# Experts with few tokens on 32 slots, chosen by a branch for each weight matrix

## The chip, the core and the metric

The kernel runs on one core of a Trainium2 chip. The metric is the device time of one execution in microseconds (us), the median of several runs. A profiled execution gives the trace that all the rows below are read from. TensorE (PE in the rows, with its weight loads as PEld) multiplies matrices into PSUM; VectorE (DVE) and ScalarE (ACT) do the work on elements; SyncE (SP) issues the transfers of weights on the DMA engines; GpSimd (POOL) does little here.

## What is computed

Two blocks over 256 tokens of width 1024, all in fp32. The first has a mixer (a short convolution and two kinds of attention) and then a mixture of 32 experts with the four best for each token; the second has a convolution and Fourier mixer, two feed-forward layers and a pooling mixer. The change lies in the experts alone:

```python
logits = (xt @ router_w + router_b).astype(jnp.float32)
top_vals, top_idx = lax.top_k(logits, TOP_K)              # 4 of 32 experts
top_w = jax.nn.softmax(top_vals, axis=-1)
combine = jnp.einsum('tk,tke->et', top_w, one_hot(top_idx, N_EXPERTS))
def expert_step(acc, params):
    w1, b1, w2, b2, gate_e = params                       # w1 [1024, 2048], w2 [1024, 1024]
    u = xt @ w1 + b1
    glu = jnp.minimum(u[:, ::2], SWIGLU_LIMIT)
    lin = jnp.clip(u[:, 1::2], -SWIGLU_LIMIT, SWIGLU_LIMIT)
    a = glu * jax.nn.sigmoid(SWIGLU_ALPHA * glu) * (lin + 1)
    return acc + gate_e[:, None] * (a @ w2 + b2), None
```

The reference runs every expert over all tokens. The kernel runs an expert over its own tokens: these are gathered into slots by a one-hot matrix, and the results are scattered back, times their weights.

## The kernel before

**Weights.** All weights come as a stream of tiles of 1 MB (8 KB on each of 128 partitions) through 19 slots (`Ring`, the loads issued at L139 on SyncE's queue). `ring.take()` hands out the next tile, `ring.release(item)` frees its slot and issues the load that takes it; that load waits on SyncE's queue until the last matmul that reads the slot is done. An expert has 12 tiles: 8 of w1, 4 of w2. So the tile 19 places further on is issued when a tile is released.

**Slots.** The main path takes the first 64 tokens of an expert (`C = 64`). `w1_mm` (L994, the bias at L999) multiplies them with the first matrix: the 64 columns of slots fill half of TensorE's columns, so two chunks of 512 weights run beside each other in two column groups; each of the 8 tiles is released when its matmuls are done (`free(k)`). `glu` (L1008 to L1012, VectorE and ScalarE) works on two banks of PSUM. `w2_mm` transposes (L1016), copies the result on ScalarE (L1017), and multiplies with the second matrix (L1026), again in two column groups, with a release for each tile.

**More than 64 tokens.** A branch on the expert's count, `tc.If(cv_e > C)` at L1139, runs the first half of a narrow path for up to 32 more tokens (`narrow_a`: `gather1` L958, `w1_mm` with n=32, `glu` of one bank), and inside it a further branch (`wide`, L1083) for more than 96. The second half (`narrow_b`, with `w2_mm32`: L1034, L1035, L1041) stands behind the branch at L1159. For the 32 slots the matmuls run in four column groups. Expert after expert all of this is written out, so the code of the skipped paths lies between. The counts are read into registers of TensorE, ScalarE and VectorE (`count`, L985).

**Order in an expert.** The branch at L1139; `gated` of the expert before (L1046 to L1048); the one-hot matrices of the next pair of experts (L952) where the expert is the first of a pair; first matrix; `glu`; the scatter of the expert before (L1055); its own scatter matrix (`scat_mat`: L973, L975, copies L976 on ScalarE and `gc` L977 on VectorE); the branch at L1159; transposes; half of the next pair's gather (`gather2`, L967, into the bank that `scat_mat` used), given to `w2_mm` as `fill`, so that it runs while ScalarE copies; second matrix. Each engine runs its own list in this order and waits on semaphores. In the last expert 10 released slots go to buffers of the second block and not to the stream.

Of the kernel before, what the change touches and what calls it, by code (L numbers as in the profile page):

```python
# [23 lines left out]
KO = (0, 2, 4, 6, 1, 3, 5, 7)  # neighbours from different banks of PSUM  # L24
# [5 lines left out]
# order of the steps of the first mixer  # L30
# [7 lines left out]
# column packs: name -> (offset, width)  # L38
# [16 lines left out]
NCOL1 = _COLS["conv_w2"][0]  # the columns before are for the first block alone  # L55
# [55 lines left out]
NKEEP = _COFF["tri_gt"][0]  # the rest is for the first block alone  # L111


class Ring:
    """a stream of weight tiles through 8 KB slots; a slot is a tag of a pool"""
# [31 lines left out]
    def release(self, item):  # L147
        """the slot takes the next load, unless a claim on slots is open"""
        if self.claim:
            self.claim -= 1  # L150
            self.claimed.append(item[0])
        else:
            self.free.append(item[0])
        self.pump()


def block_kernel(tc, a, out):
# [7 lines left out]
    # ------------------------------------------------------------------ weight stream  # L165
# [38 lines left out]
    # the last tile comes in two loads, so that its first rows are used while the others come  # L204
# [27 lines left out]
    # ------------------------------------------------------------------ resident data  # L232
# [39 lines left out]
    class Split:  # L272
        """next weight tile in two halves, each as high and low part in fp32r"""
# [37 lines left out]
    def cols_mm(ps, halves, xh, xl):  # L311
        """ps[b] = (128 columns of half b)^T x, tokens along the free axis"""
        for b, (hi, lo) in enumerate(halves):
            h3, l3 = (w.rearrange("p (k n) -> p k n", k=KT) for w in (hi, lo))
            for k in KO:
                mm3(ps[b], h3[:, k, :], l3[:, k, :], xh[:, k, :], xl[:, k, :], k == KO[0], k == KO[-1])

    def pair_mm(acc, yh, yl, kp, halves, first, last, ts=(0, 1), hs=(0, 1)):
        """acc[t][h] += y[:, tile 2 kp + j]^T (row tile j of the pair)"""
# [13 lines left out]
    # ------------------------------------------------------------------ first block: modulation, h  # L333
# [40 lines left out]
    # weights of the forget gate, padded to 32 columns  # L374
# [66 lines left out]
    # ------------------------------------------------------------------ mixer  # L441
    v_row = ap_.tile([P, 2, 768], F32, name="v_row")
    # log f of the six heads from columns 0 and 64 on
    lf = tp_.tile([P, 2, 2, 64], F32, name="lf")
    cumq = tp_.tile([P, 2, 8], F32, name="cumq")
    # queries and keys of the two heads of a pair, each on its 64 partitions; on the others a head's
    # row is chosen on the queries' side and the sums of -log f of all heads are on the keys'
# [23 lines left out]
    def head_rstd(sq, ms, n):  # L471
        """1 / rms over the 64 rows of a head, in place of the squares"""
# [23 lines left out]
    # 384 wide score tiles. stick breaking, [key, query]: 0..255 keys 0..127 against all queries,  # L496
    # 256..383 keys 128..255 against queries 128..255. forgetting, [query, key]: 0..127 the first
    # query tile against its keys, 128..383 the second against all.
# [105 lines left out]
    def fx_z(i):  # L604
# [6 lines left out]
        mk = con("mask_qk")  # of 128 keys before and the query tile's own  # L611
# [19 lines left out]
    def fx_t(i):  # L631
        """to [key, query]: 0..255 keys 0..127, 256..383 keys 128..255 of queries 128..255"""
# [49 lines left out]
    def group(g, b):  # L682
        """half b of a group of columns (of rows, for the values)"""
# [21 lines left out]
    # ------------------------------------------------------------------ output projection  # L705
# [27 lines left out]
    def row_cols(src, j0):  # L733
        """rows j0 and j0 + 1 of src, features along the partitions"""
# [9 lines left out]
    def router_cols():  # L744
        """the second norm's shift, repeated, and its gain, features along the partitions"""
# [4 lines left out]
    def router_bias(s2b, gain):  # L750
        """what the shift adds to the router's bias; the router's weights times the gain"""
# [49 lines left out]
    # ------------------------------------------------------------------ residual, second norm, router  # L801
# [7 lines left out]
    cnt = mp.tile([P, NE], I32, name="cnt")  # L809
    gate1, shift2 = rowt[:, 0, :], rowt[:, 1, :]  # L810
# [36 lines left out]
    def logits(t, hTs):  # L847
        """x times the router's weights, these times the rows' gain; 1 / rms and the rest come later"""
# [12 lines left out]
    def top4(t):  # L861
        """the largest four of a row of logits, and the exponentials"""
# [42 lines left out]
    dve.tensor_copy(cnt, pos[:, 2, :])  # L905
    act.preload_act_table_set(SET_SIG)
# [5 lines left out]
    # ------------------------------------------------------------------ experts  # L912
# [9 lines left out]
    # the halves of b2 from partitions 0 and 64 on  # L922
# [16 lines left out]
    GT_x = mo.tile([P, T], F32R, name="GT_x")  # L939
    U = mps.tile([P, 2, 512], F32, name="U")  # L940
# [3 lines left out]
    def one_hot(S, e, base, n=C):  # L944
        """token -> slot from base on, laid out 128 / n times"""
# [15 lines left out]
    def gather2(Sp, xg, q, bank=bank0):  # L961
        """row tiles 4q .. 4q+3 for two experts at once; Sp: [token, expert, t, (copy, slot)]"""
# [25 lines left out]
    def w1_mm(sel, w1s, xg, n=C, free=None):  # L988
        """u of n slots: chunk j of 512 columns on the partitions from n * (j % (128 / n)) on"""
        m = P // n  # L990
        for k in range(KT):
# [9 lines left out]
            if free:  # L1001
                free(k)

    def glu(nb, l):
        """of nb banks of u"""
# [8 lines left out]
    def w2_mm(av, w2s, ps, o_ps, free=None, fill=None):  # L1014
# [3 lines left out]
        if fill:  # L1018
            fill()
        a4 = aT_t.rearrange("p (b j c) -> p b j c", b=4, j=2)  # L1020
        for kk in range(KT):
            # hidden tile kk belongs to chunk n = kk // 2, half hb = kk % 2
# [5 lines left out]
            if free and hb:  # L1028
                free(KT + n)

    def w2_mm32(av, w2s, ps, o_ps):
        """32 slots; even and odd hidden tiles summed on partitions of their own"""
# [11 lines left out]
    def gated(o_ps, t32, gc, oh, ol):  # L1044
        """times the weights of the slots and the second gate, in two parts"""
# [11 lines left out]
    def pair_hot(p):  # L1057
        """one-hot matrices of experts 2p and 2p + 1"""
        Sp = S_all[p % 2]
        for i in range(2):  # L1060
            one_hot(Sp[:, i], 2 * p + i, 0)
        return Sp

    def bias2():
        """the gated rows of b2, weighted as the experts' outputs are"""
# [14 lines left out]
    # The first 64 tokens of an expert take the main path. Up to 32 more take a narrow one, in two  # L1080
    # steps around the main path's, and the rest goes 64 at a time.
# [25 lines left out]
    def diagonals():  # L1107
        """diag(w_j) for the taps of the second block's convolution that TensorE takes"""
# [12 lines left out]

    Sp = pair_hot(0)
# [8 lines left out]
    for e in range(NE):  # L1131
# [7 lines left out]
        with tc.If(cv_e > C):  # L1139
            # one-hot matrices that are free: the next pair's before they are made, this pair's first after its use  # L1140
            S_x = S_all[(p + 1 - b) % 2][:, 0]
            wide(C + 32, cv_e, e, S_x, sel, w1s, w2s, Oh[b], Ol[b])
            narrow_a(e, S_x, sel, w1s)
# [6 lines left out]
        w1_mm(sel, w1s, lambda k: xg2[p % 2][:, k, b, :], free=lambda i: ring.release(items[i]))  # L1150
        glu(2, l_t)
# [7 lines left out]
        with tc.If(cv_e > C):  # L1159
            narrow_b(w2s, Oh[b], Ol[b])  # L1160
        fill = (lambda: gather2(Sp, xg2[(p + 1) % 2], b)) if 2 * (p + 1) < NE else None
        w2_mm(l_t, w2s, bank1, bank1, free=lambda i: ring.release(items[i]), fill=fill)
# [469 lines left out]
```

## Time and profile before

| | us |
|---|---|
| median of 3 runs | 1738.89 |
| lowest and highest | 1734.43, 1739.25 |
| span of the profiled execution | 1734.7 |
| TensorE, busy time in it | 1583.5 |
| DMA engines, mean share over the span | 0.77 for the main queue |

The span runs from the first to the last instruction of the profiled execution; a run's time is taken from outside it. The experts take about 1020 us of the span: the first matmul of expert 0 starts at 215.1 us, and expert 31's last one ends near 1235. In the rows a busy engine is one that has an instruction under way; a name such as `U<-w,M` says what is written and read, and "128*64" with a matmul is rows times columns of the array that it uses. A letter q behind an engine (PEldq, SPq) marks its sequencer, which decodes, branches and waits.

### The profile page before, as it was taken

Reading aid. Unit: us, or ns where it says so; the run is one execution under the profiler, and the core shown is the slowest. Engines: PE = TensorE matmul, PEld = TensorE weight load, DVE = VectorE, ACT = ScalarE, POOL = GpSimd, SP = SyncE. Lnnn points to the kernel's source line nnn. Section 1 sums busy time; section 2 is a strip of 40 time slices with the busy share of each in tenths; the row PEclk is TensorE's granted clock in tenths of the full one; section 3 lists DMA queues with packets and bytes.
Section 4 is the critical chain, followed back from the end, with each engine's and each line's share of the span. In section 5 each row is a group of like instructions: output and inputs, shape, how many; then the busy total and the mean of one; then the engine's idle time right before and its main releaser. Section 6 shows DMA issues by size and latency. Waiting matters only on the chain. (4 is left out here: it accounts for less than half of the span.)

```text
span 1734.7 us, 22326 instructions
## 1 busy us (share of the span) xinstructions
PE 1583.5 (91%) x9214; PEld 955.0 (55%) x9214; DVE 576.2 (33%) x968; ACT 417.7 (24%) x660; POOL 68.9 (4%) x53
## 2 busy tenths in 40 slices
PE   5999899888989898989989899898889999999998
PEld 2877634343433333433334344343585999989997
DVE  3457401111111111021111111111496655566454
ACT  3465201000100101010101001010534543464343
POOL 0000200000000000000000000000110000200000
PEclk8999999989999999899999999999999999999999
DMA  9568899968999999969999999999224545445430
GB/s 395 229 246 316 321 354 415 414 281 322 414 414 414 417 415 415 393 268 387 416 414 414 416 392 416 415 414 408 108 97 170 214 154 216 154 161 213 178 122 25
DMA packets 95330, 535.44 MB, mean 309 GB/s; under 512 B 8352, under 2 KB 8864, under 8 KB 50976
## 3 DMA queue, kind: packets, MB, share of 16 engines
q1 hardware_dynamic: 94240, 531.37, 76.7%
q8 instruction: 142, 2.33, 0.5%
q10 hardware_dynamic: 896, 1.31, 0.2%
q14 instruction: 52, 0.43, 0.1%
HBM read 531.60 MB, written 1.05 MB: 307 GB/s over the span
## 5 line engine op out<-in xcount | busy, mean ns | idle before, releaser
L994 PE MATMUL U<-w,M 128*64 128x512 f32 (+1 forms) x2176 | 487.8, 619 | 63.9 <-PEq L1139 54.7
L994 PEld LDWEIGHTS U<-w,M 128*64 128x64 f32 (+1 forms) x2176 | 172.9, 140 | 374.6 <-issue 367.9
L1026 PE MATMUL misc<-w,aT_t 128*64 128x512 f32 x1024 | 229.5, 601 | 1.5 <-ACT aT_t L1017 0.8
L292 DVE TENSOR_TENSOR whl<-w,whl 128x1024 fp32r<-128x1024 f32 x168 | 204.2, 1272 | 54.8 <-ACT whl L289 54.7
L309 PE MATMUL G<-hTh,whl 128*128 128x256 f32 x720 | 201.5, 280 | 0.8 <-DVE whl L292 0.8
L307 PE MATMUL G<-hTh,whl 128*128 128x256 f32 x720 | 201.6, 280 | 0.1
L308 PE MATMUL G<-hTl,whl 128*128 128x256 f32 x720 | 201.2, 279 | 0.0
L289 ACT ACTIVATE whl<-w 128x1024 fp32r<-128x1024 f32 x174 | 169.8, 1045 | 21.8 <-DMA w<-in_w_in_dram 19.2
L1008 DVE TENSOR_SCALAR M<-U 128x512 f32<-128x512 f32 (+1 forms) x34 | 23.0, 676 | 444.3 <-PE U L994 427.7
L1026 PEld LDWEIGHTS misc<-w,aT_t 128*64 128x64 f32 x1024 | 71.3, 138 | 135.8 <-issue 128.7
L1009 ACT ACTIVATE M<-M 128x512 f32<-128x512 f32 (+1 forms) x34 | 21.0, 618 | 509.2 <-DVE M L1008 509.2
L1046 DVE SCALAR_TENSOR_TENSOR M<-misc,gc,g2hc 128x512 f32<-128x512 f32 x32 | 24.0, 751 | 340.1 <-PEq L1139 333.4
L307 PEld LDWEIGHTS G<-hTh,whl 128*128 128x128 f32 x720 | 135.7, 188 | 1.2 <-ACT whl L289 0.3
L309 PEld LDWEIGHTS G<-hTh,whl 128*128 128x128 f32 x720 | 135.6, 188 | 1.0 <-DVE whl L292 1.0
L308 PEld LDWEIGHTS G<-hTl,whl 128*128 128x128 f32 x720 | 135.6, 188 | 0.8
L1047 ACT ACTIVATE OO<-M 128x512 fp32r<-128x512 f32 x34 | 21.4, 630 | 283.5 <-DVE M L1046 283.5
L307 PE MATMUL Y<-hTh,whl 128*128 128x256 f32 x224 | 66.5, 297 | 6.8 <-DVE hTh L437 6.1
L309 PE MATMUL Y<-whl,gl 128*128 128x512 f32 x176 | 69.7, 396 | 0.8 <-DVE gl L1463 0.8
L307 PE MATMUL Y<-whl,gh 128*128 128x512 f32 x176 | 69.6, 395 | 0.3 <-ACT gh L1462 0.3
L308 PE MATMUL Y<-whl,gh 128*128 128x512 f32 x176 | 69.5, 395 | 0.0
L308 PE MATMUL Y<-hTl,whl 128*128 128x256 f32 x224 | 65.8, 294 | 0.7 <-DVE hTl L1235 0.7
L967 PE MATMUL misc<-S,h 128*128 128x128 f32 x512 | 65.0, 283 | 0.0
(380 smaller groups left out, 1653.8 us busy)
## 6 DMA issues: line engine op xcount, KB each, us to landing
w<-in_w_dram SPq DMA_DIRECT2D x383, 1024.0 KB, 11.6
w<-in_w_ada_dram SPq DMA_DIRECT2D x24, 1024.0 KB, 9.9
w<-in_w_gate_dram SPq DMA_DIRECT2D x22, 1024.0 KB, 5.0
w<-in_w_up_dram SPq DMA_DIRECT2D x22, 1024.0 KB, 5.4
w<-in_w_down_dram SPq DMA_DIRECT2D x22, 1024.0 KB, 5.1
w<-in_w_in_dram SPq DMA_DIRECT2D x12, 1024.0 KB, 16.4
w<-in_w_ab_dram SPq DMA_DIRECT2D x6, 1024.0 KB, 14.5
w<-in_w_out_dram SPq DMA_DIRECT2D x4, 1024.0 KB, 10.8
```

The costliest lines, as they stand in the source:

```text
L289: act.activation(self.t[j][:, 0, :], src, AF.Copy)
L292: engine.tensor_tensor(self.t[j][:, 1, :], self.w[:, 1024 * j:1024 * (j + 1)], self.t[j][:, 0, :].bitcast(F32), ALU.subtract)
L307: pe.matmul(ps, lh, rh, start=start, stop=False)
L308: pe.matmul(ps, lh, rl, start=False, stop=False)
L309: pe.matmul(ps, ll, rh, start=False, stop=stop)
L967: pe.matmul(ps[:, k], h2[:, t, kk * P:(kk + 1) * P], Sp[:, :, t, 0:C], start=(t == 0), stop=(t == 1))
L994: pe.matmul(U[o:o + n, j // m, :], xg(k), w1s[k][:, 512 * j:512 * (j + 1)], start=(k == 0), stop=(k == KT - 1), tile_position=(0, o))
L1008: dve.tensor_scalar(g, uv[:, :, :, 0], 7.0, None, ALU.min)
L1009: act.activation(s_, g, AF.Sigmoid, scale=1.702)
L1026: pe.matmul(o_ps[C * h:C * h + C, :], lhs, w2s[n][:, hb, 512 * h:512 * (h + 1)], start=(kk == 0), stop=(kk == KT - 1), tile_position=(0, C ...
L1046: dve.scalar_tensor_tensor(t32, o_ps, gc, g2hc, ALU.mult, ALU.mult)
L1047: act.activation(oh, t32, AF.Copy)
```

## The change

An expert with at most 32 tokens runs both of its matrices on 32 slots in four column groups, with the functions that the narrow path already had (`w1_mm` with n=32, `glu` of one bank, `w2_mm32`). The choice is a branch for each matrix, `tc.If(cv_e > 32)` with an `Else`, on TensorE, ScalarE and VectorE; the branch for over 64 tokens moves inside it. The tiles of a matrix are released behind the branch, all together. `gather2` stands ahead of the second branch and not between the transposes and the second matrix. The one-hot matrices lay out the slots of such an expert four times 32 and not twice 64 (`slot_of`). The narrow path has a one-hot matrix of its own (`S_x`). Comments were taken out elsewhere.

```diff
+    few = mp.tile([P, NE], F32, name="few")
...
+    dve.tensor_scalar(few, pos[:, 2, :], 32.5, -32.0, ALU.is_lt, ALU.mult)
...
+    S_x = mo.tile([P, 2, P], F32, name="S_x")
+    upper = mo.tile([P, P], F32, name="upper")
+    slot_of = mo.tile([P, P], F32, name="slot_of")
...
-    def w1_mm(sel, w1s, xg, n=C, free=None):
+    def w1_mm(sel, w1s, xg, n=C):
...
-            if free:
-                free(k)
...
-    def w2_mm(av, w2s, ps, o_ps, free=None, fill=None):
+    def w2_mm(av, w2s, ps, o_ps):
...
-        if fill:
-            fill()
...
-            if free and hb:
-                free(KT + n)
...
         for i in range(2):
-            one_hot(Sp[:, i], 2 * p + i, 0)
+            e = 2 * p + i
+            dve.scalar_tensor_tensor(slot_of, upper, few[:, e:e + 1], iota, ALU.mult, ALU.add)
+            for t in range(2):
+                dve.tensor_scalar(Sp[:, i, t, :], slot_of, posm[:, t, e:e + 1], None, ALU.is_equal)
...
+    dve.tensor_scalar(upper, iota, 31.5, None, ALU.is_gt)
...
-        with tc.If(cv_e > C):
-            S_x = S_all[(p + 1 - b) % 2][:, 0]
-            wide(C + 32, cv_e, e, S_x, sel, w1s, w2s, Oh[b], Ol[b])
-            narrow_a(e, S_x, sel, w1s)
         if e > 0:
             gated(*done)
...
-        w1_mm(sel, w1s, lambda k: xg2[p % 2][:, k, b, :], free=lambda i: ring.release(items[i]))
-        glu(2, l_t)
+        xg_e = xg2[p % 2][:, :, b, :]
+        with tc.If(cv_e > 32) as many:
+            with tc.If(cv_e > C):
+                wide(C + 32, cv_e, e, S_x, sel, w1s, w2s, Oh[b], Ol[b])
+                narrow_a(e, S_x, sel, w1s)
+            w1_mm(sel, w1s, lambda k: xg_e[:, k, :])
+            glu(2, l_t)
+        with many.Else():
+            w1_mm(sel, w1s, lambda k: xg_e[:, k, 0:32], 32)
+            glu(1, l_t)
+        for it in items[:8]:
+            ring.release(it)
...
-        with tc.If(cv_e > C):
-            narrow_b(w2s, Oh[b], Ol[b])
-        fill = (lambda: gather2(Sp, xg2[(p + 1) % 2], b)) if 2 * (p + 1) < NE else None
-        w2_mm(l_t, w2s, bank1, bank1, free=lambda i: ring.release(items[i]), fill=fill)
+        if 2 * (p + 1) < NE:
+            gather2(Sp, xg2[(p + 1) % 2], b)
+        with tc.If(cv_e > 32) as many:
+            with tc.If(cv_e > C):
+                narrow_b(w2s, Oh[b], Ol[b])
+            w2_mm(l_t, w2s, bank1, bank1)
+        with many.Else():
+            w2_mm32(l_t, w2s, bank1, bank1)
+        for it in items[8:]:
+            ring.release(it)
```

## Rows read from the trace of the kernel before

**Rows 1.** The page's first line: the span.

```profile
span 1734.7 us, 22326 instructions
```

**Rows 2.** The page, span in 40 slices: DMA busy tenths, GB/s of each.

```profile
DMA  9568899968999999969999999999224545445430
GB/s 395 229 246 316 321 354 415 414 281 322 414 414 414 417 415 415 393 268 387 416 414 414 416 392 416 415 414 408 108 97 170 214 154 216 154 161 213 178 122 25
```

**Rows 3.** Windows: stretch, length, engines' busy us (instructions), then PEclk, DMA share, GB/s.

```profile
360.00:380.00 20.00, 17.09 (x84) 10.22 (x84) 0.64 (x3) 0.77 (x2) 0.00 (x0) 0.66 0.81 331
460.00:660.00 200.00, 181.50 (x942) 76.66 (x940) 30.93 (x66) 19.24 (x34) 0.00 (x0) 0.99 1.02 415
842.00:1166.00 324.00, 294.40 (x1487) 124.39 (x1484) 51.62 (x109) 30.68 (x56) 0.00 (x0) 0.97 1.01 412
```

**Rows 4.** Waits: waiter <- releaser: us in total, times, longest; 240 to 1250, SyncE's whole.

```profile
PE U L994 <- DMA w<-in_w_dram: 4.0, 2, 2.0
...
SPq L139 <- PE U L994: 470.9, 244, 24.3
```

**Rows 5.** The loads issued at L139, from 200 to 1210 us.

```profile
DMA to landing us min/median/max: 4.8/11.8/20.1
```

**Rows 6.** Timeline of TensorE, expert 4: start, length, line, work [idle before <- releaser].

```profile
336.11 12.24 PE L994 MATMUL U<-w,M 128*64 128x512 f32 x56 [1.89 <-PEq L1139]
...
349.29 1.94 PE L994 MATMUL U<-w,M 128*64 128x512 f32 x8
351.16 1.19 PE L1055 MATMUL Y<-OO,GT 64*128 64x512 f32 x8
...
352.75 0.41 PE L975 MATMUL misc<-cst,S 128*128 128x128 f32 x2
354.15 0.66 PE L1016 MATMUL misc<-cst,M 128*128 128x128 f32 x4 [0.99 <-DVE M L1012]
354.64 1.95 PE L967 MATMUL misc<-S,h 128*128 128x128 f32 x16
356.52 7.09 PE L1026 MATMUL misc<-w,aT_t 128*64 128x512 f32 x32
```

**Rows 7.** Timeline of TensorE: narrow second matrix of expert 5; first matmuls of expert 6.

```profile
405.55 3.64 PE L1041 MATMUL misc<-w,aT_t 128*32 128x512 f32 x32 [0.47 <-ACT aT_t L1035]
...
423.87 0.87 PE L994 MATMUL U<-w,M 128*64 128x512 f32 x2 [1.98 <-DMA w<-in_w_dram]
```

**Rows 8.** Instructions of the branch lines: duration ns min/median/max, first and last start us.

```profile
L1139 PEldq COMPARE_BRANCH  x34: 70/6062/6665, 208.2 to 1200.1; - x34
L1139 PEldq EVENT_SEMAPHORE  x30: 51/51/51, 214.9 to 1206.2; - x30
...
L1159 PEldq COMPARE_BRANCH  x34: 78/332/373, 229.8 to 1221.8; - x34
...
L1083 PEldq COMPARE_BRANCH  x2: 6064/6154/6243, 359.3 to 715.5; - x2
```

**Rows 9.** Timeline of VectorE: experts 4 (two banks) and 5 (one bank).

```profile
353.40 0.69 DVE L1012 TENSOR_TENSOR M<-M 128x512 f32<-128x512 f32 x1
354.01 0.19 DVE L981 COPY sel<-cst 128x64 f32<-128x64 f32 x1
354.11 0.15 DVE L977 COPY gc<-misc 128x1 f32<-128x1 f32 x1
...
385.56 0.42 DVE L1008 TENSOR_SCALAR M<-U 128x256 f32<-128x256 f32 x1 [10.01 <-PE U L994]
...
387.26 0.42 DVE L1012 TENSOR_TENSOR M<-M 128x256 f32<-128x256 f32 x1 [0.49 <-DVE M L1011]
```

**Rows 10.** Timeline of TensorE: first expert's first matrix, last expert's second matrix.

```profile
215.14 14.32 PE L994 MATMUL U<-w,M 128*64 128x512 f32 x56 [4.83 <-PEq L1139]
...
1228.01 7.09 PE L1026 MATMUL misc<-w,aT_t 128*64 128x512 f32 x32 [0.75 <-ACT aT_t L1017]
```

## The prediction

> **What bounds the kernel now.** I read the span first [rows 1], then the DMA lines of the page [rows 2]: from the sixth to the 28th of 40 slices, some 1000 us, the queues move about 415 GB/s with all engines full, but for two dips. That is the expert stage, and it looks like a stream of weights that nothing in the arithmetic can shorten. The windows say the same [rows 3]: 415 and 412 GB/s in two long undisturbed stretches, so a tile of 1.049 MB comes every 2.53 to 2.55 us and an expert's 12 tiles every 30.4 to 30.6 us.
>
> The waits correct this [rows 4]. TensorE lost 4.0 us in all to weights that had not landed, while SyncE's queue stood 470.9 us behind the first matrix's matmuls (L994) alone, waiting for slots to come free. A tile takes a median of 11.8 us from issue to landing [rows 5], hence four or five of the 19 slots are in flight and the rest hold landed tiles. TensorE is the bound, and the stream is only just slower than it: a usual expert, read from one start of L994 to the next idle gap, takes 336.11 to 363.61, then 1.89 us idle [rows 6]: 27.5 + 1.9 = 29.4 us against 30.5 for its tiles. TensorE stays behind the stream because each of the two experts with over 64 tokens throws it back by some 30 us (the second matrix ends at 363.61, the next expert starts at 423.9 [rows 7]; during that the queues fall to 331 GB/s [rows 3]).
>
> So two floors lie close together. Whatever TensorE saves pays until the stream is the bound.
>
> How many experts change path can't be read from the trace. I evaluated the reference's router on its inputs: 19 experts have at most 32 tokens, 13 have more, two of these over 64 (65 and 81, experts 5 and 16), and the trace shows the narrow path exactly twice (L1083 x2 [rows 8]).
>
> **Cost of a small expert (at most 32).** Its matmuls exist already, in the narrow path. The second matrix for 32 slots took 3.64 us [rows 7] instead of 7.09 [rows 6], at full clock. The first has twice the records: 2 x 3.64 = 7.3, with its bias 0.9 more, 8.2 us instead of 15.1 (336.11 to 351.23). Behind it the order changes: the gather of the next pair (`gather2`, 1.95) now stands ahead of the branch, and its bank is free only when `gc` is copied, which VectorE does after `glu`. One bank of `glu` ends 2.1 us after the matmuls (385.56 to 387.68 [rows 9]); with sel and gc (0.3) and the branch's end on VectorE (unknown; between 0.1 and 0.9, taken 0.5) the gather starts at 2.9, the time that scatter and the scatter matrix (2.0) fill only partly. Then 1.9 of gather, 0.33 for a near branch (L1159 [rows 8]), 0.4 transposes, 0.5 to the copy's end, 3.64: 9.7 us. Start to end 8.2 + 9.7 = 17.9 instead of 27.5, a gain of 9.6 us.
>
> **What that gives back: the far branch.** On TensorE the branch at L1139, over the code of the wide and narrow paths, took a median of 6.06 us [rows 8]; the near one at L1159, over the second half of the narrow path, 0.33. Only 1.9 of the 6.06 shows as idle time [rows 6], since the sequencer ran 4.3 us ahead of the matmuls (the branch of expert 5 began at 359.3 [rows 8], its predecessor's matmuls ended at 363.61). A 32-slot second matrix empties the same queue in half the time, so the lead is about 2.2 and the gap 4.0. If the end of the else part waits for its matmuls (the skipped block ends in such a wait, 30 times [rows 8]), the gap is the full 6.06 + 0.3 = 6.4. Between these I take 5.2, 3.3 more than now. After a gap of that size the clock is at the lower of its levels: the first expert, after 4.83 us idle, needed 14.32 for what otherwise takes 12.24 [rows 6, 10], 2.1 us lost; I charge 1.9. Net: 9.6 - 3.3 - 1.9 = 4.4 us, times 19 = **84 us saved**.
>
> The Trainium skill gives a compare-and-branch about 108 ns (Advanced Engine Details and Errata, Control Flow Timing). By that figure no gap would be left and the saving would stop at the stream's floor (below); the 6.06 us row disagrees and decides.
>
> **Cost of the 13 larger experts.** Nothing of theirs gets shorter. Now 5.3 us pass from the end of the first matrix to the start of the second (351.23 to 356.52), because the gather covered ScalarE's copy. Moved ahead it waits for `gc`: two banks of `glu` end at 2.9, gather from 3.7 to 5.6, the inner branch 0.33, transposes 0.66, copy 0.6: 7.2, so +1.9; the jump over the else part adds at most 0.33. 2.2 x 13 = **29 us lost**.
>
> **Releases.** All 8 slots of the first matrix now come free at its end, up to 13.4 us later than the first of them did, and the 4 of the second likewise. In the queue of SyncE nothing but such loads follows. Cover: 11 other slots, 11 x 2.55 = 28 us of stream. It is gone at the start (the ring is full, so DMA stands idle some 7 us longer until 225) and behind the two experts over 64. I carried the rule through expert by expert (a tile is issued when the tile 19 before it is released, lands 2.55 after its predecessor and no sooner than 4.8 after issue [rows 5]); TensorE then waits for tiles mainly in runs of small experts. I charge 5 us, bounds 0 and 15.
>
> VectorE's three new kinds of operation (`few`, `upper`, one `slot_of` per expert, each 0.2 to 0.3 like its neighbours) fall while it waits for L994, but for the first pair, under 1 us. `S_x` of its own removes no wait that shows. One price is unseen and bounded both ways: the shorter or longer PE code could shift what a branch finds loaded; the rows give 0.33 and 6.06, and I take 0.33 for the new inner branches, being of the size of L1159's.
>
> **Sum.** -84 + 29 + 5 = -50 us. The second matrix of the last expert ends at 1235.1 now [rows 10], and what follows is TensorE's own work with its weights early, so the span goes from 1734.7 to 1684.7. The median of the runs, 1738.89, is 4.2 above that span; forecast **1689 us**.
>
> **Rivals.** (1) *The stream becomes the bound.* If the gaps stay under cover, DMA runs without a stop from the first release: 8.2 + 1.9 after 215.14, first landing at 230, 364 tiles x 2.55 = 928, the last at 1158, end of the stage at 1159.5, 75.6 us earlier: 1663. For it: both floors are close. Against it: the 6.06 us row. (2) *Dear gaps.* Every small expert pays the full 6.4 (+1.2 x 19 = 23), and the larger ones that follow start at the low clock (about 10 x 1.7 = 17), with VectorE's end at 0.9 (0.4 x 32, partly hidden, 6): +46, 1735. (3) *The branch ahead of the second matrix is far as well*: a small expert there jumps over the second half of the narrow path and the 64-slot matmuls, about twice the code that L1159 skips now. Then 6.06 instead of 0.33 stands in each small expert, of which the gather's queued 1.9 hides part: +4 us, and 1.7 of low clock: 5.7 x 19 = 108, 1797, slower than before. The point from which it decides is 50 / 19 = 2.6 us per small expert. For it: the code to be skipped grows. Against it: all 34 branches at L1159 took 0.37 at most. (4) *It doesn't do what it says* and every expert takes the longer path: 32 x 2.2 = 70, 1809. The counts speak against it.
>
> Rival 3 is what the Trainium skill would lead one to: a taken branch whose target is outside a window of two pages makes the sequencer fetch before it goes on (Runtime: NRT & Kernel Launch, Instruction fetch mechanics). L1139 agrees with that; whether the new jump stays within the window no row shows.
>
> **How the numbers follow.** Chances: forecast (1670 to 1710) 0.50; rival 1 0.17; rival 2 0.18; rival 3 0.12; rival 4 0.03. About 0.3% (5 us) can be told from no change. Rival 2 ends within it in a quarter of its cases: faster 0.81, same 0.04, slower 0.15. The range leaves out rivals 3 and 4: 1660 (tiles at 2.53 us, rival 1) to 1735 (rival 2).
>
> **What would show it.** Right: 19 second matrices of about 3.6 us beside 13 of 7.1; far branches still near 6 us, one per expert, with gaps of 4 to 6.4 us after small experts and about 2 after larger ones; near ones under 0.5; the end of the last second matrix near 1185; TensorE's waits for weights up from 4 us to some tens. Wrong: waits for weights over 100 us (the stream binds, rival 1); a second group of branches near 6 us per small expert (rival 3); idle time before the gather beyond 1 us in small experts (VectorE's chain is longer than I took); stretches at half clock through whole matrices rather than at their start.

## The result, and the profile after

The changed kernel takes 1693.51 us in the median (four runs, 1690.06 to 1696.69), the kernel before 1736.66 beside it: a ratio of 0.9771, 95% interval 0.9745 to 0.9797 (the two medians alone give 0.9752). The forecast was 1689 us, its range 1660 to 1735. The profiled execution's span went from 1734.7 to 1694.9 us. The second matrix of the last expert, which ended at 1235.1 [rows 10], ends at 1191.4.

The page's first line, then its busy share and rate of the DMA engines in 40 slices, to be laid beside [rows 1, 2]:

```profile
span 1694.9 us, 22352 instructions
...
DMA  9668899986999999999999999999724554435430
GB/s 394 232 233 326 334 364 388 415 351 237 410 414 415 412 415 414 414 390 409 414 415 381 399 415 414 415 415 413 315 90 149 208 214 171 178 149 219 154 125 26
```

The first dip (351 and 237 GB/s, expert 5) is still there; the second, 268 GB/s before, has become 390. The timeline of TensorE shows the first small expert of an undisturbed stretch (expert 7, 23 tokens) and the beginning of a larger one (expert 8); columns as in [rows 6]:

```profile
448.82 6.21 PE L999 MATMUL U<-w,M 128*32 128x512 f32 x56 [3.56 <-issue]
...
455.96 1.06 PE L999 MATMUL U<-w,M 128*32 128x512 f32 x8
...
459.73 2.05 PE L972 MATMUL misc<-S,h 128*128 128x128 f32 x16 [0.66 <-DVE gc L982]
461.62 0.38 PE L1033 MATMUL misc<-cst,M 128*128 128x128 f32 x2
462.74 3.64 PE L1040 MATMUL misc<-w,aT_t 128*32 128x512 f32 x32 [0.74 <-ACT aT_t L1034]
470.44 13.93 PE L999 MATMUL U<-w,M 128*64 128x512 f32 x56 [4.06 <-DVEq L1151]
...
490.40 2.05 PE L972 MATMUL misc<-S,h 128*128 128x128 f32 x16 [1.20 <-DVE gc L982]
492.60 0.63 PE L1019 MATMUL misc<-cst,M 128*128 128x128 f32 x4
```

From 448.82 to 457.02 the first matrix takes 8.2 us, and the second ends 9.4 us later, at 466.38: 17.6 us, where the forecast had 17.9. Then come 4.06 us of idle time ahead of the larger expert, 3.56 ahead of the small one. What ends these is not the same, and the waits of TensorE tell it (240 to 1250 us; SyncE's over the whole span):

```profile
PE U L999 <- issue: 60.1, 18, 9.0
PEld U L999 <- DVEq L1151: 37.5, 8, 5.3
PE U L999 <- DMA w<-in_w_dram: 29.7, 14, 3.8
PE U L999 <- DVEq L1151: 27.4, 7, 4.4
PEld U L999 <- DMA w<-in_w_dram: 23.7, 34, 2.3
...
SPq L139 <- DMA w<-in_w_dram: 321.0, 190, 3.3
SPq L139 <- PE U L999: 256.5, 141, 27.4
```

Set against [rows 4], three things have moved. TensorE waits for tiles, 29.7 us in its matmuls, from 4.0. SyncE's queue stands less behind the first matrix (256.5 us, before 470.9) and much behind the loads themselves (321.0): slots come free faster than tiles land. And a wait is there that the forecast did not have: seven larger experts' first matrix waits for VectorE's sequencer, which comes late to its inner branch (L1151). The branches, as in [rows 8]:

```profile
L1150 PEldq COMPARE_BRANCH  x45: 70/306/7393, 208.9 to 1158.1; - x45
L1151 PEldq COMPARE_BRANCH  x15: 70/6072/7284, 233.0 to 1078.0; - x15
...
L1170 PEldq COMPARE_BRANCH  x45: 70/224/4003, 227.9 to 1180.2; - x45
L1171 PEldq COMPARE_BRANCH  x15: 71/218/352, 259.4 to 1104.7; - x15
```

Of the 45 records at L1150 and at L1170, 32 each are the branch itself, one for each expert: the 19 small experts jump at it and the 13 larger ones go on. The other 13 are the larger ones' jumps over the else part, and with them the median at L1150 is low. Taken one by one, the 19 jumps of small experts there are far (5.95 to 7.39 us), and so are 11 at L1151 (6.01 to 7.28), one in each of the 30 experts that skip the code for over 64 tokens. Of the 19 jumps of small experts at the second branch, L1170, three are long (3.93, 4.00 and 2.57 us).

Last the windows, as in [rows 3]: two stretches within expert 5 (373.75 to 422.75 us) in which the stream hardly moves and stands still, and three that cover most of the rest of the stage:

```profile
380.00:392.00 12.00, 11.12 (x72) 3.10 (x66) 1.61 (x4) 0.42 (x1) 0.00 (x0) 1.00 0.30 101
412.00:418.00 6.00, 4.38 (x24) 2.00 (x26) 0.69 (x1) 1.18 (x2) 0.00 (x0) 1.00 0.00 0
...
430.00:660.00 230.00, 181.68 (x1160) 71.64 (x1152) 37.67 (x94) 20.93 (x42) 0.00 (x0) 0.94 1.02 414
800.00:1000.00 200.00, 164.67 (x924) 66.76 (x920) 31.62 (x74) 18.37 (x36) 0.00 (x0) 0.93 1.00 404
1000.00:1189.00 189.00, 141.88 (x926) 50.62 (x920) 29.82 (x75) 18.07 (x39) 0.00 (x0) 0.94 1.02 414
```

TensorE is busy in 182 of 230 us from 430 on while the DMA engines are full, where in 460 to 660 before it was busy in 181.5 of 200 [rows 3]. Counting tiles of the stage from 0, tile 88 (in expert 7) lands at 427.9 and the last at 1189.5, 2.0 us before the last second matrix ends: 295 tiles in 761.6 us, 2.58 each, with no step of over 4.6 us between two landings. In the kernel before, the last tile landed at 1200.8, 34.3 us before the last second matrix ended; the change has used up nearly all of this distance, and the stream itself ends only 11.3 us sooner. So behind the seventh expert the stream looks like what ends last, and TensorE's sum, on which the forecast was built, like a close second. The experiments had to tell whether that is so.

### The profile page after: what moved, and what is told of

The parts are those of the page before. It is cut to its first block, busy times and chain, and to the rows that moved or that the text cites. A ratio compares the mean times of both kernels' runs of the same rounds, so it can differ in the third digit from the quotient of the medians.

```text
span 1694.9 us, 22352 instructions
## 1 busy us (share of the span) xinstructions
PE 1433.6 (85%) x9176; PEld 878.3 (52%) x9176; DVE 571.0 (34%) x1002; ACT 408.6 (24%) x660; POOL 69.0 (4%) x53
## 5 line engine op out<-in xcount | busy, mean ns | idle before, releaser
L999 PE MATMUL U<-w,M 128*32 128x512 f32 (+1 forms) x2176 | 385.7, 671 | 133.9 <-issue 64.5
L999 PEld LDWEIGHTS U<-w,M 128*32 128x32 f32 (+1 forms) x2176 | 114.4, 132 | 401.1 <-issue 336.2
L1011 DVE TENSOR_SCALAR M<-U 128x256 f32<-128x256 f32 (+1 forms) x34 | 17.9, 526 | 463.8 <-PE U L999 463.8
L1012 ACT ACTIVATE M<-M 128x256 f32<-128x256 f32 (+1 forms) x34 | 17.0, 499 | 528.0 <-DVE M L1011 528.0
L1027 PE MATMUL misc<-w,aT_t 128*64 128x512 f32 x416 | 92.1, 595 | 9.7 <-ACT aT_t L1020 9.7
L1040 PE MATMUL misc<-w,aT_t 128*32 128x512 f32 x672 | 82.8, 614 | 17.4 <-ACT aT_t L1034 14.1
L972 PE MATMUL misc<-S,h 128*128 128x128 f32 x512 | 72.0, 299 | 27.1 <-DVE gc L982 26.3
L972 PEld LDWEIGHTS misc<-S,h 128*128 128x128 f32 x512 | 65.6, 208 | 35.6 <-DVE gc L982 33.2
```

The costliest lines, as they stand in the source:

```text
L972: pe.matmul(ps[:, k], h2[:, t, kk * P:(kk + 1) * P], Sp[:, :, t, 0:C], start=(t == 0), stop=(t == 1))
L999: pe.matmul(U[o:o + n, j // m, :], xg(k), w1s[k][:, 512 * j:512 * (j + 1)], start=(k == 0), stop=(k == KT - 1), tile_position=(0, o))
L1027: pe.matmul(o_ps[C * h:C * h + C, :], lhs, w2s[n][:, hb, 512 * h:512 * (h + 1)], start=(kk == 0), stop=(kk == KT - 1), tile_position=(0, C ...
L1040: pe.matmul(o_ps[o:o + 32, :], aT_t[:, lo:lo + 32], w2s[n][:, hb, 512 * h:512 * (h + 1)], start=(n == 0), stop=(n == 3), tile_position=(0, o))
```

## The experiments

Theory S: from the seventh expert on the weight stream ends last, so only less data, a faster rate or an earlier seventh expert shorten the time. Theory T: TensorE's sum ends last, as forecast, and its waits for tiles only fill what it would lose anyway. Ratios are to the kernel before in the same comparison; a difference of two ratios carries 0.004 to 0.005 of uncertainty (their intervals added as squares), 7 to 9 us.

### Which of the two ends last

**Fewer tiles, the same arithmetic.** The last tile of an expert's second matrix is left out and the one before it read in its place, in every third expert from 8 on; in the second kernel in each from 8 to 30 (the step of 3 becomes 1):

```diff
-        for kp in range(4):
+        for kp in range(3 if e >= 8 and (e - 8) % 3 == 0 and e < NE - 1 else 4):
             pairs(a["w2"][e], kp)
```

> The changed kernel with eight weight tiles less to load: in experts 8, 11, ... 29 the last tile of the second matrix is not loaded, and its matmuls read the tile before it instead (left out: those eight tiles; TensorE's work is the same). Theory S (the weight stream ends last from the seventh expert on): 8 tiles by 2.58 us less, 1671 to 1677 us. Theory T (TensorE's sum ends last, its 54 us of waits for weights behind the seventh expert being slack that something else would fill): 1688 to 1696 us. Between the two, 1678 to 1687 us, would mean that the two are within some 15 us of one another.

> The same with 23 tiles less, one in each of experts 8 to 30. The stream alone would give 23 by 2.58 us less, 59 us; TensorE waits for weights 54 us behind the seventh expert in the changed kernel (22.6 on the matmuls, 31.5 on the weight loads, which may overlap). Theory S: TensorE's own sum takes over some 23 to 54 us below the changed kernel, 1640 to 1671 us, with its waits for weights nearly gone and idle stretches in the stream again. Theory T: no change, 1688 to 1696 us. If the stream were still what ends last, 1632 to 1638 us.

Eight tiles less gave 1678.95 us, ratio 0.9683 (0.9651 to 0.9714): 0.0088 of 1736 us, 15 us below the changed kernel, between the two theories. 23 tiles less gave 1677.51, ratio 0.9675 (0.9643 to 0.9706): 17 us below, hardly more, and above the range that S gave for it (1640 to 1671). With eight tiles less the last tile still lands 1.1 us before the last second matrix ends, and TensorE's waits for weights behind 430 us are what they were, 58.6 us over all lines against 58.3. With 23 less the last tile lands 13.9 us before that end, the stream has pauses again, and the waits are 31.0 us. On the first matrix they were, in the changed kernel and then with 23 tiles less (430 to 1192 us):

```profile
PE U L999 <- DMA w<-in_w_dram: 22.6, 12, 3.5
PEld U L999 <- DMA w<-in_w_dram: 21.2, 30, 2.3
```

```profile
PE U L999 <- DMA w<-in_w_dram: 16.3, 4, 9.1
PEld U L999 <- DMA w<-in_w_dram: 11.1, 22, 0.8
```

```profile
660.00:800.00 140.00, 105.97 (x704) 43.42 (x697) 21.25 (x54) 11.94 (x25) 0.00 (x0) 0.87 0.90 358
800.00:1000.00 200.00, 161.33 (x904) 62.32 (x900) 31.22 (x70) 17.33 (x33) 0.00 (x0) 0.93 0.95 378
```

So S holds for the changed kernel, but by a thin margin: TensorE's own sum ends some 16 us earlier, and takes over when the stream is lightened by more than that.

**Less arithmetic, the same tiles.** One kernel never takes the path for over 64 tokens (the first edit, at both inner branches), the other takes the small path for every expert up to 64 (the second, at both outer ones):

```diff
-            with tc.If(cv_e > C):
+            with tc.If(cv_e > 200):
```
```diff
-        with tc.If(cv_e > 32) as many:
+        with tc.If(cv_e > C) as many:
```

> The changed kernel with the branches for over 64 tokens taken only above 200, so never: the code and the far branch stay, the tokens beyond 64 of experts 5 and 16 are left out. Theory S: what goes is the DMA's idle time behind expert 5 (two gaps, some 20 us) and nothing of expert 16's: 17 to 22 us faster than the changed kernel, 1672 to 1677. Theory T: both narrow paths of TensorE go, 2 x 29 us: 55 to 62 us faster, 1632 to 1638.

> The changed kernel with the small path for all experts of up to 64 tokens, so that tokens beyond 32 of eleven experts are left out: TensorE has 9 us less to do in each of the eleven. Theory S: only the two of them ahead of expert 5 can pay, and they pay by starting expert 5 sooner: 5 to 15 us faster than the changed kernel, 1679 to 1689, with tiles landing every 2.55 to 2.58 us from the first release on. Theory T: 11 x 9 = 100 us faster, about 1595.

Without the path for over 64: 1664.97 us, ratio 0.9608 (0.9565 to 0.9652), 28 us below the changed kernel; tile 88 lands at 403.1 instead of 427.9, and that is 25 of them. With the small path for all: 1671.46, ratio 0.9646 (0.9601 to 0.969), 22 us below and not 100; tile 88 at 406.2 is again 22 of them, and the rate behind it stays at 2.57 us per tile. Both gains lie above what S had priced (17 to 22 us and 5 to 15): tile 88 came sooner than it had reckoned, and why isn't shown. In the second kernel TensorE's waits for tiles grew instead (240 to 1250 us):

```profile
PEld U L999 <- DMA w<-in_w_dram: 108.7, 83, 2.4
PE U L999 <- DMA w<-in_w_dram: 59.7, 45, 3.7
```

A gain of 22 us where T had 100 is against T. It also shows where time can still be had: in the first seven experts, where TensorE holds the stream up.

**No far branch.** The code for over 64 tokens is taken out of the changed kernel, branches and all.

> The changed kernel without the code for tokens beyond 64 (left out: those tokens of experts 5 and 16, as in the run with that path never taken). The jump on 32 tokens is then over little code and should be near, so the 6 us of the far one are gone in some 45 crossings of the loop. Theory S (the weight stream ends last): 1656 to 1665 us, at most some 9 us below the run with the path never taken (1665.0), the last expert's tile still landing within 8 us of the last second matrix's end. Theory T (TensorE's sum ends last, so each far jump counts whatever it hides behind): some 2 to 4 us in each of 32 experts less, 1540 to 1600 us.

1645.49 us, ratio 0.9485 (0.9465 to 0.9504), some 20 us below the kernel that only never takes that path, which S had put at 9 at most. The branch is near now, TensorE waits for tiles through the whole stage, and the DMA engines have no pause:

```profile
L1150 PEldq COMPARE_BRANCH  x45: 70/231/1069, 207.2 to 1112.2; - x45
```

```profile
PEld U L999 <- DMA w<-in_w_dram: 331.7, 191, 3.3
PE U L999 <- DMA w<-in_w_dram: 132.5, 156, 2.4
```

Tile 88 lands at 392.9 (10 us earlier than with the branch only never taken), and the 295 behind it come every 2.54 us instead of 2.57 (another 10 us). Fewer bytes of instructions can be part of that: the page of the profile counts 1.84 MB on the two instruction queues, and 3.10 MB with the code in place and never taken; at the stream's rate the difference is some 3 us. The rest of the better rate isn't explained. So the code for over 64 tokens costs the changed kernel some 28 us where it runs, in two experts, and some 20 us more where it is skipped.

### Parts of the change, alone, on the kernel before

**Releases at the end of each matrix.** No branch, no 32 slots:

```diff
-        w1_mm(sel, w1s, lambda k: xg2[p % 2][:, k, b, :], free=lambda i: ring.release(items[i]))
+        w1_mm(sel, w1s, lambda k: xg2[p % 2][:, k, b, :])
         glu(2, l_t)
+        for it in items[:8]:
+            ring.release(it)
```
(and the same for the four tiles of the second matrix)

> One part of the change alone, on the kernel before: the tiles of a matrix are released together behind its last matmul, with no new branch and no 32-slot path. In the kernel before TensorE's sum ends last and the stream has stretches of idle time, so theory S (a late release costs only where the stream is what ends last) expects no change within 4 us, 1733 to 1741 us, with the stream's idle stretches moved and not lengthened. The rival, that late releases are themselves paid for in full (the prediction's term of 5 us, with its upper bound of 15), expects 1742 to 1752 us.

1730.65 us, ratio 0.9977 (0.9947 to 1.0008): no difference that can be told. Where TensorE ends last, late releases cost nothing that shows (1.4 us by the upper end of the interval); the stream's pauses in the seventh to tenth slices stay as they were.

**The gather ahead of the second branch.**

```diff
+        if 2 * (p + 1) < NE:
+            gather2(Sp, xg2[(p + 1) % 2], b)
         with tc.If(cv_e > C):
             narrow_b(w2s, Oh[b], Ol[b])
-        fill = (lambda: gather2(Sp, xg2[(p + 1) % 2], b)) if 2 * (p + 1) < NE else None
```

> Another part alone, on the kernel before: the gather for the next pair moves out of the stretch between the transposes and the second matrix to a place ahead of the second branch, as in the changed kernel; no 32-slot path, tiles are released one by one. Theory: the longer way from the first matrix to the second in the larger experts (6.7 to 8.2 us in the changed kernel, 5.3 before) comes from the gather's new place, some 1.2 to 1.9 us in each of 31 experts, and TensorE's sum ends last here: 1774 to 1796 us. Rival: it comes from the new branch on 32 tokens, and the gather hides behind the glu: 1733 to 1745 us.

1783.91 us, ratio 1.029 (1.0234 to 1.0346): 50 us slower, by the place of the gather alone, 16 matmuls in an expert. Its expert 4, beside [rows 6]:

```profile
359.64 0.42 PE L975 MATMUL misc<-cst,S 128*128 128x128 f32 x2
361.21 2.05 PE L967 MATMUL misc<-S,h 128*128 128x128 f32 x16 [1.15 <-DVEq L1161]
363.41 0.63 PE L1016 MATMUL misc<-cst,M 128*128 128x128 f32 x4
364.79 7.09 PE L1026 MATMUL misc<-w,aT_t 128*64 128x512 f32 x32 [0.75 <-ACTq L1083]
```

The gather now stands where TensorE waits first 1.15 us for VectorE and later 0.75 us for ScalarE's copy, which it used to cover; first to second matrix takes 6.66 us instead of 5.29. Over the 30 experts that have a gather (the last pair has none) that is 41 of the 50 us; the rest wasn't traced. In the changed kernel the larger experts pay it too, 6.72 us in seven of the eleven and 8.2 in four. In these four the granted clock was 0.50 during the gather (259.5 to 262.9 us in expert 1), which took about 3.5 us and not 2.05; the wait of 1.20 us ahead of it is the same in the others. Expert 1's gather:

```profile
259.13 3.46 PE L972 MATMUL misc<-S,h 128*128 128x128 f32 x16 [1.20 <-DVE gc L982]
```

### Where the code lies

**The branch for over 64 tokens back outside, ahead of the gating.** The idea was to spare the larger experts their wait for VectorE:

```diff
+        with tc.If(cv_e > C):
+            wide(C + 32, cv_e, e, S_x, sel, w1s, w2s, Oh[b], Ol[b])
+            narrow_a(e, S_x, sel, w1s)
         if e > 0:
             gated(*done)
...
         with tc.If(cv_e > 32) as many:
-            with tc.If(cv_e > C):
-                wide(C + 32, cv_e, e, S_x, sel, w1s, w2s, Oh[b], Ol[b])
-                narrow_a(e, S_x, sel, w1s)
```

> The changed kernel with the branch for over 64 tokens put back ahead of the gating of the expert before, as it stood at first; all else is as changed. In the changed kernel the inner branch stands on VectorE behind that gating (2.7 us) and, for every second expert, behind the next pair's one-hot matrices, and TensorE's first matmul of a larger expert waits for it: 65 us in 15 waits in the trace. Theory S (from the seventh expert on the weight stream ends last): the idle gap ahead of larger experts falls from about 4.1 to about 2.2 us, but only those before tile 88 pay: 2 to 8 us faster than the changed kernel, so 1686 to 1692. Theory T (TensorE's sum still ends last): 11 larger experts by 2 us, 20 to 25 us faster, 1668 to 1674. A rival within both: the outer branch, now jumping over less code, adds a second near branch, 0.3 us for each expert, and takes half of it back under T.

1724.38 us, ratio 0.9941 (0.9915 to 0.9968): both theories missed, and 30 us of the gain are gone. The two branches in a row, and the gap ahead of a small expert that met both:

```profile
L1143 PEldq COMPARE_BRANCH  x34: 70/6074/7433, 206.7 to 1191.6; - x34
```

```profile
L1153 PEldq COMPARE_BRANCH  x45: 70/218/5693, 213.3 to 1197.9; - x45
```

```profile
458.61 7.93 PE L999 MATMUL U<-w,M 128*32 128x512 f32 x56 [9.26 <-DMA w<-in_w_dram]
```

Behind the far branch of 6 us, eight of the 19 jumps of small experts over the 64-slot first matrix were long as well (the other records of L1153 are the larger experts'): 2.8 us once, 5.5 to 5.7 us seven times, 42 us together, and the gaps ahead of those seven experts are 9.2 to 9.5 us, where those ahead of all others of up to 64 tokens are 2.1 to 4.1. This is rival 3's mechanism, a second far branch, in another place than the forecast had looked for it. Nested, as in the changed kernel, an expert passes one far branch only.

**The same code, moved.** The changed kernel has two gaps that no wait explains, 7.58 us ahead of expert 2 and 9.02 ahead of expert 18:

```profile
278.87 3.64 PE L999 MATMUL U<-w,M 128*32 128x512 f32 x16 [7.58 <-issue]
```

```profile
792.54 2.79 PE L999 MATMUL U<-w,M 128*32 128x512 f32 x12 [9.02 <-issue]
```

The far branch ahead of expert 2 ends at 273.1, one weight load runs at 273.30, and the next only at 278.87, with its tile landed since 236.9. To move the code, the gathers ahead of expert 0 were written out twice and three times:

```diff
         gather2(Sp, xg2[0], q, (bank0, bank1)[q])
+        gather2(Sp, xg2[0], q, (bank0, bank1)[q])
```

> The changed kernel with its code moved a little: the two gathers ahead of expert 0 are written out twice (same values), so that everything behind them on TensorE stands further on; they run some 2 to 4 us once, ahead of the stage. The changed kernel has two gaps that stand out, 7.6 us ahead of expert 2 and 9.0 us ahead of expert 18, where the first weight load of L999 runs at the branch's end and the second one only 5.5 and 5.3 us later, with no wait for a semaphore between them and the tile landed 20 us before. Theory F (the code behind the jump's target isn't there yet, by where it happens to lie): these two gaps shrink to the usual 2 to 4 us, or such gaps appear ahead of other experts; time 1682 to 1706 us by how many are met. Theory R (something of these experts themselves, or of the releases): both gaps stay as they are, 7 to 9 us, no others appear, 1693 to 1698 us.

> The same with the two gathers written out three times. Theory F: again another set of experts with such gaps; the sum of the gaps ahead of the first matrices, 143 us in the changed kernel, moves by 5 us or more against the other shift or against no shift. Theory R: both gaps stay at experts 2 and 18 and the sum stays within 3 us.

1683.27 us, ratio 0.9725 (0.9683 to 0.9768), and 1683.6, ratio 0.9719 (0.9678 to 0.9761): with work added, both were some 10 us faster in the median than the changed kernel (by the ratios 8 and 9 us, about the uncertainty of such a difference). The sum of the gaps ahead of the first matrices fell from 143 to 127.3 and 119.7 us. Both gaps are gone; in the first of the two:

```profile
275.36 6.22 PE L999 MATMUL U<-w,M 128*32 128x512 f32 x56 [3.43 <-issue]
```

```profile
780.02 8.97 PE L999 MATMUL U<-w,M 128*32 128x512 f32 x56 [3.60 <-issue]
```

Pauses of 4.4 to 5.6 us between two weight loads of one line, in the stage: five in the changed kernel (at 273, 360, 619, 787 and 1139 us, 25.8 us together), three in the first shift (at 495, 545 and 644), two in the second (527 and 1050). Each begins within 1.3 us of the end of a far branch. Shorter ones of 2.6 to 3.6 us there are two, two and none. They follow the place of the code and not the expert, as theory F has it; that the sequencer is waiting for code in them is inferred, for the trace shows no wait at all. Those ahead of the seventh expert delay the stream (tile 88 lands at 417.4 and 420.4 instead of 427.9).

The Trainium skill (Runtime: NRT & Kernel Launch, Instruction fetch mechanics) says that a taken branch to a target outside the fetched window has to fetch first, and the runs agree (6 us with the skipped code in place, 0.2 to 1.1 without it). It also says that going on past the end of a block is mostly hidden; right behind such a jump the runs show 4.4 to 5.6 us for a stop that may be that, which no trace shows.

### Releases in halves, and VectorE's wait

The first matrix was split into two branches of four tiles, with four slots released behind each; then, besides, the one-hot matrices of the next pair were put ahead of the gating:

```diff
-            w1_mm(sel, w1s, lambda k: xg_e[:, k, :])
+            w1_mm(sel, w1s, lambda k: xg_e[:, k, :], C, range(4))
         with many.Else():
-            w1_mm(sel, w1s, lambda k: xg_e[:, k, 0:32], 32)
+            w1_mm(sel, w1s, lambda k: xg_e[:, k, 0:32], 32, range(4))
+        for it in items[:4]:
+            ring.release(it)
+        with tc.If(cv_e > 32) as many:
...
```
```diff
+        if b == 0:
+            S_pair = Sp
+            if e + 2 < NE:
+                Sp = pair_hot(p + 1)
         if e > 0:
             gated(*done)
-        if b == 0:
...
```

> The changed kernel with the first matrix in two branches of four tiles each, and four slots released behind each: the price of releasing at the end. Theory S: DMA idles less at the start (the first release comes 4.5 us sooner) and behind the expert with 65 tokens (four slots 7 us sooner), and every us of that is won at the end: 8 to 12 us faster than the changed kernel, 1682 to 1686. Theory T: nothing is won, and one near branch more for each expert costs 0.2 to 0.4 us, 32 times: 6 to 13 us slower, 1700 to 1707.

> The run with the first matrix in two branches of four tiles each, and besides, the two one-hot operations for the next pair ahead of the gating of the expert before, so that VectorE comes to its inner branch some 1.8 us earlier in the seven even-numbered larger experts, whose gap ahead of the first matrix is 4.0 to 4.4 us against 2.1 to 2.5 us in the others. Theory S (the stream ends last): TensorE's earlier start only meets a tile that hasn't landed, 1679 to 1685 us, beside 1684.8 us for the halves alone. Theory T (TensorE's sum): 7 times 1.9 us less, 1668 to 1673 us.

1684.77 us, ratio 0.9728 (0.9693 to 0.9764), and 1684.33, ratio 0.9709 (0.9689 to 0.9729), the second 11 us below the changed kernel. Both hit what S expected. But the split moves the code too: the two pauses ahead of experts 2 and 18 are gone in both, and one ahead of expert 28 is new (gaps of 9.45 and 9.23 us). So how much of this belongs to earlier releases stays open; that tile 88 lands at 411.2 and 414.2, before that of either shift, speaks for a part of it. Six of the larger experts have an even number, not seven, and the one-hot matrices' new place shortened only the gaps ahead of three of them, those that follow another larger expert (4.0 to 4.4 us; to 2.4 in two). Nothing came of it in the time, as S has it for a wait in a stretch that the stream ends.

## Why the prediction was right, and where it was not

The stage can be cut up by the first and the last matmul of each matrix. Sums in us over the 32 experts; the gaps run from one expert's second matrix to the next one's first, and the last column is the kernel with 23 tiles less, in which TensorE waits for tiles about half as long (its profile was taken at 1669.64 us, below its median of 1677.51, and that of the changed kernel at 1696.69, above its own):

| | before | after | difference | forecast | 23 tiles less, difference |
|---|---|---|---|---|---|
| 19 small experts, first matrix to end of second | 539.7 | 391.9 | -147.8 | -146 | -162.2 |
| 11 experts of 33 to 64 tokens | 309.3 | 343.0 | +33.7 | +29 | +31.8 |
| 2 experts over 64 | 94.3 | 97.9 | +3.5 | (in that) | +2.1 |
| gaps | 76.6 | 143.2 | +66.6 | +63 | +62.8 |
| stream | | | (in all of them) | +5 | |
| together | 1020.0 | 976.0 | -43.9 | -50 | -65.6 |

(Differences are of unrounded times. The forecast's -146 is 19 times 9.6 less the 1.9 of the low clock; its 63 is 19 times 3.3.)

**The small expert**, where nothing else stands in its way, was right in each step: 8.2 us for the first matrix, 9.4 instead of 9.7 behind it. The granted clock was low for a part of twelve of the 19 first matrices; in the four of these without a wait inside (experts 0, 6, 17 and 18) the 56 first records of L999 take 7.6 to 7.9 us instead of 6.2 (charged 1.9). All 19 first matrices together took 200.9 us, 45 more than 19 times 8.2, where 36 had been charged for the clock: waits for tiles and pauses are in that too. That the row of the table agrees to 2 us is therefore partly luck. The working took 27.5 us for such an expert before, 522.5 for all, and they had 539.7; it put them at 376 after, and they have 391.9.

**The far branch** was the step that decided, and it held: about 6 us, one per expert. Its gap was put too high: 3.4 to 3.8 us between two small experts in the usual case, under the lower of the two ends (4.0), so the wait at the end of the else part, on which the upper end rested, doesn't show. Over 16 gaps behind small experts that is +34.9 us, not 53. The sum of all gaps agreed nevertheless, because others grew that the forecast left alone: by 14.8 us ahead of the two experts over 64 (17.06 and 18.51 us from the second matrix before them to their narrow first, 11.26 and 9.48 before; 8.1 us of it without a cause but code, L963 waiting for issue), by 7.4 between larger experts, by 5.7 ahead of expert 2.

**The larger experts** lost 1.97 us between their matrices (21.7 over 11), where 2.2 were charged. The gather alone showed the cause of 1.37 of them, and the low clock during the gather in four of the eleven (1.5 us each) makes up most of the rest. What was missed is the branch on VectorE. The forecast named no engine but TensorE as waiting at the new inner branch; VectorE comes to it behind the gating and, in an expert of even number, behind the one-hot matrices, which end at 849.85 in this row of its timeline, while TensorE had been free since 845.93:

```profile
846.03 0.75 DVE L1045 SCALAR_TENSOR_TENSOR M<-misc,gc,g2hc 128x512 f32<-128x512 f32 x1 [10.82 <-PE misc L1027]
...
849.37 0.48 DVE L1064 TENSOR_SCALAR S<-slot_of,posm 128x128 f32<-128x128 f32 x2
```

Behind such a gap the clock is mostly low there too (a granted 0.84 to 0.91 over the first matrix in nine of the eleven, but 1.00 in expert 3 behind 3.78 us): 12.0 us more in the first matrices of the eleven, some of it waits for tiles, which the forecast had only in rival 2.

**The stream** is the term that was mis-sized. The charge of 5 us was for late releases, and those cost nothing that shows where they were tried alone on the kernel before; what they cost in the changed kernel stays open (the releases in halves). What cost was the stream itself: TensorE's own sum fell by at least 56 us (by the ratio of the kernel with 23 tiles less) to 65 (in the profiles, the last column) and not 50, and the stream took 16 to 22 us of that back. So the forecast's mechanism, TensorE's sum, was right in its large terms and not what ended last. The two misses had opposite signs, and that the time came out within 5 us of the forecast is luck in that part. Rival 1 had the mechanism, but let it run from the first release without a pause at 2.55 us: in fact TensorE set the pace up to tile 88, with the DMA engines idle within expert 5 (101 and 0 GB/s in the windows above), and the 295 tiles behind came every 2.58 us. That the waits stayed under 100 us, the forecast's sign against rival 1, was no sign: they were 53 us on the first matrix, and the stream bound.

**Rivals 2 to 4.** The dear gaps didn't come, nor the longer path for all. Rival 3's second far branch showed at L1170 in three of 19 small experts and not in all, and came in eight of 19 in the kernel with the branch back outside.

## What to carry to other kernels

When a saving exceeds the distance to the next floor, forecast the two floors side by side, and from the point on where each begins: here the stream could only bind from where TensorE had last made it pause. A branch that several engines take is reached by the last of them, so list what stands ahead of it on each. And where code is skipped, its length is a cost: one far jump per expert, nested and not in a row, and code whose place decides over gaps of 5 us.

## What the runs showed of the hardware

- A jump over the long skipped code took 6 us on TensorE's sequencer, at times 7.2 to 7.5; a second jump right behind it, over a 64-slot first matrix, took 0.2 us in eleven of 19 cases, 2.8 in one and 5.5 to 5.7 in seven; and none at the first branch took over 1.1 us once the long code was gone.
- Behind such a jump TensorE's weight loads can stop once more for 4.4 to 5.6 us after the first of them, with no wait in between that the trace shows. Adding instructions ahead of the stage moved these stops, and both kernels with added work were 8 to 9 us faster by the ratios, about the uncertainty of each.
- With all DMA engines full a tile of 1 MB came every 2.58 us behind the seventh expert of the changed kernel, and every 2.54 without the code for over 64 tokens. A load took a median of 19.9 us from issue to landing there (427 to 1190 us), against 11.8 before [rows 5]: at nearly the same rate, some eight loads were under way (19.9 / 2.58) and not four or five.
